# A seventh pair of weight rows as seven block products in each down projection

## The chip, the cores and the metric

The kernel runs on one core of a Trainium2 chip. The metric is the time of one execution on the device in microseconds (us); of several executions the median is given. The engines are named as in the profile: PE is TensorE (matmuls, with its weight loads as PEld), DVE is VectorE, ACT is ScalarE, POOL is GpSimd and SP is SyncE, which here only issues transfers.

## The reference

A trunk of two layers works on one sequence of 256 rows and 1024 columns, all in float32. Each layer adds half of a feed-forward network (FFN), then a mixer, then half of a second FFN. Four FFNs are therefore computed, each with 2816 hidden columns:

```python
def swiglu(x, w_gate, w_up, w_down):
    return (jax.nn.silu(x @ w_gate) * (x @ w_up)) @ w_down
...
for layer in range(DEPTH):
    h = h + 0.5 * swiglu(rms_norm(h, ffn1_norm[layer]), ...)
    hn = rms_norm(h, mix_norm[layer])
    ...
    h = h + 0.5 * swiglu(rms_norm(h, ffn2_norm[layer]), ...)
return rms_norm(h, final_norm)
```

Layer 0's mixer is attention over dilated windows beside a gated position mixing; layer 1's is causal attention. Neither is touched by the change.

## The kernel before

**Precision.** A float32 product is built from three matmuls of a shorter format: each operand is split into a high part and a low part, and high x high, high x low and low x high are summed (`mm3`, L236 to L239). A weight chunk is split on the chip: ACT writes the high part (`whi`, L93), DVE subtracts it from the raw weights and gets the low part (`wlo`, L94).

**The stream of weights.** `Stream` hands out weight chunks of 1 MB in a fixed order. A chunk is loaded into one of three `raw` buffers, split into one of four pairs of `whi` and `wlo`, used by PE and freed. `pump` loads and splits as far ahead as these buffers allow; it is called by `take` and by `free`. The code gives an order of instructions and their dependences; a scheduler then orders each engine's list by priority and by what it takes to be ready, so operations of one chunk can stand between those of another. A buffer is taken when any of its kind is free.

**An FFN.** For each pair of hidden tiles (128 hidden columns each, named by its first tile: 0, 2, ..., 20), `colwise` computes gate and up from the normalised input `xTh`, `xTl` (L391 to L393). `gated` makes `hm` (L674), and `keep` splits it into `hTh`, `hTl` (L242, L243). Then `project` computes the down projection: 11 chunks, one per pair, in the order of `DOWN`. A chunk has two tiles of 128 weight rows by 1024 columns, and the output has two row blocks of 128 rows (t = 0, 1) and two halves of 512 columns (h = 0, 1).

**Plain and mixed pairs.** A plain pair needs 2 x 2 x 2 = 8 block products of 128 x 128 by 128 x 512 (`part`, L458, L459, L462). A pair in `MIXED` takes 7 (`mixed_part`, `mm3`), after the scheme of Winograd: a pair is a 2 x 2 product of blocks, and with sums of blocks on both sides seven products do. The sums on the left are built in the gate/up loop by `mix_rows` (L718 to L721) and split into `seh`, `sel`. Those on the right are built from the weights in `split_mixed`: four sums (L103, L106 to L108) in `wx`, of which three are split into `wxh` and `wxl`. There is one `wx`, one `wxh` and one `wxl`, so the next mixed chunk can only write them when PE has done the products of the one before. For that reason the seven products alternate: in even mixed chunks the three that need `wxh`, `wxl` come first, in odd ones last.

**The end of a projection.** The last two chunks (four tiles) form the tail. For t = 0 they are computed for both halves, `n0.add` adds them to the residual `x` (L269), the mean square is taken (L278, L283) and POOL makes `rstd` (L249). While PE computes t = 1, `n0.scale` and the transposes (L342) put the normalised input of the next phase into `xTh`, `xTl`. Four products of the mixed chunks have banks of their own; `onto` adds them to `x` (L433 to L444), for t = 1 behind the mean of t = 0. In the next FFN and in layer 1's mixer the second block's transposes come after seven of the first eight steps of `rowwise` (L381 to L383).

Of the kernel before, what the change touches and what calls it, by code (L numbers as in the profile page):

```python
# [10 lines left out]
F32 = mybir.dt.float32  # L11
F32R = mybir.dt.float32r
# [4 lines left out]
D = 1024  # L17
NT = S // 128
KD = D // 128
# [8 lines left out]
RAW, SPL = 3, 4  # L28
PAIRS = 3
HEAT = 9  # L30
DOWN = [4, 6, 8, 0, 10, 12, 2, 14, 16, 18, 20]
MIXED = (6, 8, 10, 12, 14, 16)


LINE, SHIFT = 64, 16
# [3 lines left out]
class Stream:  # L39


    def __init__(self, nc, pools):
        self.nc, (self.raw_pool, self.hi_pool, self.lo_pool) = nc, pools
        self.specs, self.raws, self.parts = [], {}, {}
        self.loaded = self.split = self.done = self.next = self.mixes = 0

    def add(self, src, nk, w, shift=0, pieces=2, mixed=False):
        self.specs.append((src if isinstance(src, tuple) else (src,), nk, w, 4 if len(self.specs) < 2 else 2 if len(self.specs) < 6 else 1, shift,
                           0 if mixed else pieces))
# [45 lines left out]

    def split_mixed(self, j, raw, hi, lo):
        nc = self.nc
        lead = self.mixes % 2 == 0
        self.mixes += 1
        b11, b12, b21, b22 = (raw[:, i * 512 : (i + 1) * 512] for i in range(4))  # L100
        wx = self.mix_pool.tile([128, 3, 512], F32, name="wx")
        wxh, wxl = (self.mix_pool.tile([128, 3, 512], F32R, name=m) for m in ("wxh", "wxl"))
        nc.vector.tensor_sub(wx[:, 0, :], b22, b12)  # L103
        if not lead:
            self.split_piece(hi[:, 1024:], lo[:, 1024:], raw[:, 1024:])
        nc.vector.tensor_sub(b12, b12, b11)  # L106
        nc.vector.tensor_add(wx[:, 1, :], wx[:, 0, :], b11)
        nc.vector.tensor_sub(wx[:, 2, :], b21, wx[:, 1, :])  # L108
        if lead:
            self.split_piece(wxh, wxl, wx)  # L110
            self.split_piece(hi[:, 1024:], lo[:, 1024:], raw[:, 1024:])
        self.split_piece(hi[:, :1024], lo[:, :1024], raw[:, :1024])
        if not lead:
            self.split_piece(wxh, wxl, wx)
        self.parts[j] += (wxh, wxl)

    def pump(self):
        n = len(self.specs)
        while True:
            if self.loaded < n and self.loaded - RAW < self.split:  # L120
                self.load_one()
            elif self.split < self.loaded and self.split - SPL < self.done:
                self.split_one()
            else:
                break
# [24 lines left out]
def trunk(ctx: ExitStack, tc: tile.TileContext, a, out):  # L150
    nc = tc.nc
    x = a["x"][0]

    cp = ctx.enter_context(tc.tile_pool(name="cp", bufs=1))
    wk = ctx.enter_context(tc.tile_pool(name="wk", bufs=2))
    xp = ctx.enter_context(tc.tile_pool(name="xp", bufs=1))
# [6 lines left out]
    def bank():  # L163
        return ps.tile([128, 512], F32, name="bank")

    st = Stream(nc, (raw_pool, hi_pool, lo_pool))


    def add_cols(m, c0, w, pieces=2):
        n = CH // w  # L170
        for k in range(0, KD, n):
            st.add(m[k * 128 : (k + n) * 128, c0 : c0 + w], n, w, SHIFT if w == 256 else 0,
                   pieces if len(st.specs) > 1 else 4)

    def add_ffn(wg, wu, wd):
# [7 lines left out]
        for c in range(first, FF, 256):  # L183
            for m in (wg, wu):
                add_cols(m, c, 256)
        add_rows(wd, DOWN, MIXED)

    def add_rows(m, order, mixed=()):
        for k in order:
            st.add(m[k * 128 : (k + 2) * 128, :], 2, D, mixed=k in mixed)  # L190
# [210 lines left out]
    def project(tiles, order, nfinal, factor, nxt, after=None, mixed={}):  # L401
# [5 lines left out]
        def started(t, h):  # L407
            first = (t, h) not in begun
            begun.add((t, h))
            return first  # L410

        def mixed_part(k, w):
            i = list(mixed).index(k)
            e = [[v[:, j, :] for v in mixed[k]] for j in range(3)]
            a = [[[v[:, k + j, t, :] for v in tiles] for t in range(NT)] for j in range(2)]
            b = [[[v[:, j, h * 512 : (h + 1) * 512] for v in w[:2]] for h in range(2)] for j in range(2)]
            x = [[v[:, j, :] for v in w[2:]] for j in range(3)]
            own = [((0, 0), a[1][0], b[1][0]), ((0, 1), e[2], b[1][1]), (1, a[0][0], b[0][0]), (5, e[0], b[0][1])]
            sums = [(7, a[0][1], x[0]), (6, e[1], x[1]), ((1, 0), a[1][1], x[2])]
            for key, s, m in sums + own if i % 2 == 0 else own + sums:  # L420
                single = type(key) is int
                if key not in banks:
                    banks[key] = bank()
                first = i == 0 if single else started(*key)
                mm3(banks[key], *s, *m, first, single and i == len(mixed) - 1)
            if i < len(mixed) - 1:
                return
            p1, p5, p6, p7 = (banks[j] for j in (1, 5, 6, 7))
            x = [[xr[t][:, h * 512 : (h + 1) * 512] for h in range(2)] for t in range(NT)]
            u = st.mix_pool.tile([128, 3, 512], F32, name="wx")  # L430

            def onto(xs, v):
                nc.vector.scalar_tensor_tensor(xs, v, factor, xs, op0=ALU.mult, op1=ALU.add)  # L433

            onto(x[0][0], p1)
            nc.scalar.copy(u[:, 0, :], p1)
            nc.vector.tensor_add(u[:, 0, :], p6, u[:, 0, :])
            nc.vector.tensor_add(u[:, 1, :], p5, u[:, 0, :])
            onto(x[0][1], u[:, 1, :])

            def second_rows():
                nc.vector.tensor_add(u[:, 2, :], p7, u[:, 0, :])
                onto(x[1][0], u[:, 2, :])
                nc.vector.tensor_add(u[:, 1, :], p5, u[:, 2, :])  # L444
                onto(x[1][1], u[:, 1, :])

            late.append(second_rows)
# [16 lines left out]
        head = order[: len(order) - nfinal]  # L464
        w = None
        for i, k in enumerate(head):
            if i % 2 == 0:
                w = st.take()
            if k in mixed:
                mixed_part(k, w)  # L470
            elif k - 1 not in mixed:
                for t in range(NT):
                    part(t, k, w, i % 2, (0, 1))
            if i % 2 == 1:
                st.free()
            if after:
                after(i)
# [7 lines left out]
        for h, i in [(h, 2 * c + i) for c in range(2) for h in range(2) for i in range(2)] if after else \  # L485
                [(h, i) for h in range(2) for i in range(4)]:
            k = tail[i]
# [14 lines left out]
        with tc.issue_after(mean.ins):  # L502
            for f in () if last else late:
                f()
        if last:
            n0.final()
            rest = bank()
            for q, (c0, c1) in enumerate(((0, 512), (512, 768), (768, D))):
                b = rest[:, :256] if q == 2 else banks[1, q]
                for i, k in enumerate(tail):  # L510
                    w = [u[:, i % 2, c0:c1] for u in ws[i // 2]]
                    mm3(b[:, : c1 - c0], th[:, k, 1, :], tl[:, k, 1, :], *w, q == 2 and i == 0, k == order[-1])
                n1.last_add(q, slice(c0, D if q else c1), b, factor)
            n1.final(384)
            return
# [142 lines left out]
    def ffn(phase, begin=None):  # L658
        with ExitStack() as pools:
# [32 lines left out]
            def turn_all():  # L692
                for f in todo:
                    f()
                todo.clear()
# [19 lines left out]
            def mix_rows(k, hm):  # L715
                a11, a21, a12, a22 = (hm[:, i * 128 : (i + 1) * 128] for i in range(4))
                e = fp.tile([128, 512], F32, name="sil", bufs=2)[:, :384].rearrange("p (j c) -> p j c", j=3)
                nc.vector.tensor_add(e[:, 0, :], a21, a22)  # L718
                nc.vector.tensor_sub(a21, a11, a21)  # L719
                nc.vector.tensor_sub(e[:, 1, :], e[:, 0, :], a11)  # L720
                nc.vector.tensor_sub(e[:, 2, :], a12, e[:, 1, :])  # L721
                mixed[k] = [mq.tile([128, 3, 128], F32R, name=f"{n}{k}") for n in ("seh", "sel")]
                split(*mixed[k], e)

            if begin:
# [5 lines left out]
            else:  # L731
# [2 lines left out]
                block(1)  # L734
                finish(1)
            mq = st.mix_pool = pools.enter_context(tc.tile_pool(name="mq", bufs=1))
            mixed = {}
            for k in range(6 if begin else 2, FT, 2):
                ps2 = []
                for _ in range(2):  # L740
                    p = bank()
# [7 lines left out]
                hm = gated(*ps2)  # L749
                if k in MIXED:  # L750
                    mix_rows(k, hm)
                keep(k, hm)

            turn_all()
            project(hT, [k + j for k in DOWN for j in range(2)], 4, 0.5, phase + 1, mixed=mixed)


# [262 lines left out]
    Norm(0, 0)  # L1020
    Norm(1, 0)
    ffn(0, begin)
    ab_mixer(1)
    ffn(2)
    ffn(3)
    c_mixer(4)
# [49 lines left out]
```

## Time and profile before

| what | value |
|---|---|
| time, median of 3 runs | 925.27 us (924.82 to 926.18) |
| the profiled execution's own time | 924.85 us |
| its span | 923.1 us |
| instructions | 15780 |
| HBM read | 173.73 MB, 189 GB/s over the span |
| mixed pairs per down projection | 6 of 11 |

The span runs from the first to the last instruction; the time also holds the start and the end of the program. A row of a timeline gives the start in the span, the duration, the engine, the line, the tile written and those read, the shapes and, in brackets, how long the engine was idle before it and what released it. Matmuls and DVE operations overlap with the ones behind them, so the step from one start to the next is shorter than the duration. A group's row gives the count, the busy time in us and the mean of one in ns.

### The profile page before, as it was taken

Reading aid. Unit: us, or ns where it says so; the run is one execution under the profiler, and the core shown is the slowest. Engines: PE = TensorE matmul, PEld = TensorE weight load, DVE = VectorE, ACT = ScalarE, POOL = GpSimd, SP = SyncE. Lnnn points to the kernel's source line nnn. Section 1 sums busy time; section 2 is a strip of 40 time slices with the busy share of each in tenths; the row PEclk is TensorE's granted clock in tenths of the full one; section 3 lists DMA queues with packets and bytes.
Section 4 is the critical chain, followed back from the end, with each engine's and each line's share of the span. In section 5 each row is a group of like instructions: output and inputs, shape, how many; then the busy total and the mean of one; then the engine's idle time right before and its main releaser. Section 6 shows DMA issues by size and latency. Waiting matters only on the chain.

```text
span 923.1 us, 15780 instructions
## 1 busy us (share of the span) xinstructions
PE 915.7 (99%) x6442; PEld 843.2 (91%) x6442; DVE 691.9 (75%) x1044; ACT 538.2 (58%) x842; POOL 35.5 (4%) x53
## 2 busy tenths in 40 slices
PE   9999999999999999999999999999999999999997
PEld 8999998889889999988899999888989799999886
DVE  6886779977657566879876678898656575677797
ACT  6754555585867455546664555556756674555552
POOL 0000000000000000000000000000323100000000
PEclk9999999999999999999999999999999999999999
DMA  9885554757526766536486665473744457665351
GB/s 324 270 275 182 186 180 141 270 175 249 167 91 191 221 185 195 192 131 242 153 274 185 195 207 179 162 243 129 250 150 146 129 167 225 203 204 185 137 182 45
DMA packets 125704, 175.79 MB, mean 190 GB/s; under 512 B 3264, under 2 KB 104768, under 8 KB 125632
## 3 DMA queue, kind: packets, MB, share of 16 engines
q1 hardware_dynamic: 123952, 172.60, 57.5%
q10 hardware_dynamic: 1680, 2.19, 0.8%
q8 instruction: 50, 0.82, 0.4%
q14 instruction: 22, 0.18, 0.1%
HBM read 173.73 MB, written 1.05 MB: 189 GB/s over the span
## 4 chain that ended last, share of the span: by engine, by line
PE 99%; issue 1%; DVE 0%; ACT 0%; POOLq 0%; POOL 0%
PE bank L391 18%; PE bank L393 18%; PE bank L392 18%; PE bank L458 5%; PE bank L462 5%; PE bank L459 5%; PE bank L239 4%; PE bank L237 4%; PE bank L238 4%; PE bank L381 3%; PE bank L383 3%; PE bank L382 3%; PE bank L822 1%; PE bank L782 1%; PE bank L342 1%; PE bank L810 1%
## 5 line engine op out<-in xcount | busy, mean ns | idle before, releaser
L93 ACT ACTIVATE whi<-raw 128x1024 fp32r<-128x1024 f32 (+1 forms) x336 | 329.0, 1029 | 238.8 <-PE bank L392 102.8
L94 DVE TENSOR_TENSOR wlo<-raw,whi 128x1024 fp32r<-128x1024 f32 (+1 forms) x336 | 385.1, 1184 | 84.3 <-ACT whi L93 83.7
L391 PE MATMUL bank<-xTh,whi 128*128 128x256 f32 x1440 | 399.7, 278 | 0.0
L393 PE MATMUL bank<-xTh,wlo 128*128 128x256 f32 x1440 | 398.2, 277 | 0.0
L392 PE MATMUL bank<-xTl,whi 128*128 128x256 f32 x1440 | 398.2, 276 | 0.0
L391 PEld LDWEIGHTS bank<-xTh,whi 128*128 128x128 f32 x1440 | 270.3, 188 | 1.3 <-issue 1.2
L392 PEld LDWEIGHTS bank<-xTl,whi 128*128 128x128 f32 x1440 | 270.8, 188 | 0.1
L393 PEld LDWEIGHTS bank<-xTh,wlo 128*128 128x128 f32 x1440 | 270.5, 188 | 0.0
L674 DVE TENSOR_TENSOR hm<-sil,bank 128x512 f32<-128x512 f32 x38 | 26.1, 687 | 57.2 <-PE bank L393 57.1
L458 PE MATMUL bank<-whi,hTh 128*128 128x512 f32 x152 | 59.8, 393 | 0.0
L459 PE MATMUL bank<-wlo,hTh 128*128 128x512 f32 x152 | 59.2, 390 | 0.0
L242 ACT ACTIVATE hTh<-hm 128x512 fp32r<-128x512 f32 x39 | 24.5, 627 | 50.1 <-DVE hm L719 38.9
L462 PE MATMUL bank<-whi,hTl 128*128 128x512 f32 x152 | 51.4, 389 | 0.0
L94 DVE TENSOR_TENSOR wxl<-wx,wxh 128x1536 fp32r<-128x1536 f32 x24 | 42.1, 1755 | 11.3 <-ACT wxh L93 11.2
L381 PE MATMUL bank<-whi,xTh 128*128 128x512 f32 x112 | 44.4, 397 | 0.0
L383 PE MATMUL bank<-whi,xTl 128*128 128x512 f32 x112 | 43.8, 391 | 0.0
L382 PE MATMUL bank<-wlo,xTh 128*128 128x512 f32 x112 | 43.6, 390 | 0.0
L93 ACT ACTIVATE wxh<-wx 128x1536 fp32r<-128x1536 f32 x24 | 35.5, 1481 | 11.6 <-DVE wx L108 7.7
L249 POOL TENSOR_TENSOR rstd<-ms,half_neg 128x1 f32<-128x1 f32 x14 | 8.1, 582 | 797.2 <-DVE ms L283 792.9
L462 PEld LDWEIGHTS bank<-whi,hTl 128*128 128x128 f32 x152 | 28.5, 188 | 6.0
L459 PEld LDWEIGHTS bank<-wlo,hTh 128*128 128x128 f32 x152 | 28.6, 188 | 5.6
L458 PEld LDWEIGHTS bank<-whi,hTh 128*128 128x128 f32 x152 | 28.6, 188 | 5.5
(165 smaller groups left out, 1150.5 us busy)
## 6 DMA issues: line engine op xcount, KB each, us to landing
raw<-in_ffn_w_down SPq DMA_DIRECT2D x44, 1024.0 KB, 5.0
raw<-in_ffn_w_gate SPq DMA_DIRECT2D x38, 1024.0 KB, 5.5
raw<-in_ffn_w_up SPq DMA_DIRECT2D x38, 1024.0 KB, 5.4
raw<-in_c_w_in SPq DMA_DIRECT2D x12, 1024.0 KB, 5.4
raw<-in_ab_w_in SPq DMA_DIRECT2D x10, 1024.0 KB, 5.4
raw<-in_ffn_w_up SPq DMA_DIRECT2D x12, 512.0 KB, 6.5
raw<-in_ffn_w_gate SPq DMA_DIRECT2D x8, 512.0 KB, 4.0
raw<-in_ab_w_out SPq DMA_DIRECT2D x4, 1024.0 KB, 5.0
```

The source lines that it names most:

```text
L93: self.nc.scalar.activation(hi, raw, AF.Copy)
L94: self.nc.vector.tensor_sub(lo, raw, hi.bitcast(F32))
L237: nc.tensor.matmul(p, sh, mh, start=start, stop=False)
L381: nc.tensor.matmul(p, xh, w[0][:, k, :], start=k0 + k == 0, stop=False)
L382: nc.tensor.matmul(p, xh, w[1][:, k, :], start=False, stop=False)
L383: nc.tensor.matmul(p, xl, w[0][:, k, :], start=False, stop=k0 + k == KD - 1)
L391: nc.tensor.matmul(p, h, xh, start=k == 0, stop=False)
L392: nc.tensor.matmul(p, h, xl, start=False, stop=False)
L393: nc.tensor.matmul(p, l, xh, start=False, stop=k == KD - 1)
L458: nc.tensor.matmul(banks[t, h], sh, w[0][:, kw, cs], start=first, stop=False)
L459: nc.tensor.matmul(banks[t, h], sh, w[1][:, kw, cs], start=False, stop=False)
L462: nc.tensor.matmul(banks[t, h], sl, w[0][:, kw, cs], start=False, stop=last)
```

## The change

- `MIXED` gets pair 18, so seven of the eleven pairs take seven products. `DOWN` puts pair 4, a plain one, into the tail in its place, and 6 at the front.
- The four sums on the right become three operations: one subtraction over two blocks at a time, one addition, one subtraction. The order inside a chunk is the same in all: the sums, the second half of the chunk, the first half, the split of the sums.
- `wxh` and `wxl` have two homes, used in turn: tiles of their own (`near`), and the memory of `xTh` and `xTl` (`far`), which PE reads until the last gate/up product. `held` keeps the first chunk that needs `far` from being split until the gate/up loop has been written out (`open`).
- The order of the seven products no longer alternates: the four that need no sums of weights come first.
- After the last mixed chunk of a projection, the split of one more chunk (the second one of the next phase) is put off (`later`) until behind the mean of t = 0. The edge behind the mean binds the operations on DVE.
- Pair 6's left sums live in a buffer named `xn` of the pool `wk`, which the norms also use.

```diff
-DOWN = [4, 6, 8, 0, 10, 12, 2, 14, 16, 18, 20]
-MIXED = (6, 8, 10, 12, 14, 16)
+DOWN = [6, 0, 8, 10, 12, 2, 14, 16, 18, 4, 20]
+MIXED = (6, 8, 10, 12, 14, 16, 18)
...
     def split_mixed(self, j, raw, hi, lo):
         nc = self.nc
-        lead = self.mixes % 2 == 0
+        b11, b12, b21, _ = (raw[:, i * 512 : (i + 1) * 512] for i in range(4))
+        wx = self.mix_pool.tile([128, 3, 512], F32, name="wx")
+        wxh, wxl = self.mix_tiles[self.mixes % 2]()
         self.mixes += 1
...
-        nc.vector.tensor_sub(wx[:, 0, :], b22, b12)
-        if not lead:
-            self.split_piece(hi[:, 1024:], lo[:, 1024:], raw[:, 1024:])
-        nc.vector.tensor_sub(b12, b12, b11)
-        nc.vector.tensor_add(wx[:, 1, :], wx[:, 0, :], b11)
-        nc.vector.tensor_sub(wx[:, 2, :], b21, wx[:, 1, :])
-        if lead:
-            self.split_piece(wxh, wxl, wx)
-            self.split_piece(hi[:, 1024:], lo[:, 1024:], raw[:, 1024:])
+        nc.vector.tensor_sub(wx[:, :2, :], raw.rearrange("p (a b c) -> p a b c", a=2, b=2)[:, :, 1, :],
+                             raw[:, :1024].rearrange("p (a c) -> p a c", a=2))
+        self.split_piece(hi[:, 1024:], lo[:, 1024:], raw[:, 1024:])
+        nc.vector.tensor_add(b12, wx[:, 1, :], b11)
+        nc.vector.tensor_sub(wx[:, 2, :], b21, b12)
         self.split_piece(hi[:, :1024], lo[:, :1024], raw[:, :1024])
-        if not lead:
-            self.split_piece(wxh, wxl, wx)
+        self.split_piece(wxh, wxl, wx)
         self.parts[j] += (wxh, wxl)
+
+    def held(self):
+        return self.later or not self.specs[self.split][-1] and self.mixes % 2 and not self.open
...
-            elif self.split < self.loaded and self.split - SPL < self.done:
+            elif self.split < self.loaded and self.split - SPL < self.done and not self.held():
                 self.split_one()
...
-            own = [((0, 0), a[1][0], b[1][0]), ((0, 1), e[2], b[1][1]), (1, a[0][0], b[0][0]), (5, e[0], b[0][1])]
-            sums = [(7, a[0][1], x[0]), (6, e[1], x[1]), ((1, 0), a[1][1], x[2])]
-            for key, s, m in sums + own if i % 2 == 0 else own + sums:
+            for key, s, m in (((0, 0), a[1][0], b[1][0]), ((0, 1), e[2], b[1][1]), (1, a[0][0], b[0][0]),
+                              (6, e[1], b[0][1]), (5, e[0], x[0]), (7, a[0][1], x[1]), ((1, 0), a[1][1], x[2])):
...
             if i % 2 == 1:
+                st.later = bool(mixed) and i == len(head) - 1
                 st.free()
...
         with tc.issue_after(mean.ins):
             for f in () if last else late:
                 f()
+            if st.later:
+                st.later = False
+                st.pump()
...
-                mixed[k] = [mq.tile([128, 3, 128], F32R, name=f"{n}{k}") for n in ("seh", "sel")]
+                if k == MIXED[0]:
+                    both = wk.tile([128, D], F32, name="xn").bitcast(F32R)
+                    mixed[k] = [both[:, c : c + 384].rearrange("p (j c) -> p j c", j=3) for c in (0, 384)]
+                else:
+                    mixed[k] = [mq.tile([128, 3, 128], F32R, name=f"{n}{k}") for n in ("seh", "sel")]
...
+            st.mixes, st.open = 0, False
+
+            def near():
+                return [mq.tile([128, 3, 512], F32R, name=n) for n in ("wxh", "wxl")]
+
+            def far():
+                return [xp.tile([128, KD, NT, 128], F32R, name=n).rearrange("p k t c -> p (k t c)")[:, :1536]
+                        .rearrange("p (j c) -> p j c", j=3) for n in ("xTh", "xTl")]
+
+            st.mix_tiles = near, far
...
             turn_all()
+            st.open = True
```

More of the change, by code (lines that the diff above doesn't have):

```diff
@@ L45, in __init__ @@
         self.loaded = self.split = self.done = self.next = self.mixes = 0
+        self.open = self.later = False
     def add(self, src, nk, w, shift=0, pieces=2, mixed=False):
@@ L97, in split_mixed @@
         nc = self.nc
-        lead = self.mixes % 2 == 0
+        b11, b12, b21, _ = (raw[:, i * 512 : (i + 1) * 512] for i in range(4))
+        wx = self.mix_pool.tile([128, 3, 512], F32, name="wx")
+        wxh, wxl = self.mix_tiles[self.mixes % 2]()
         self.mixes += 1
[L100 to L103, printed above, removed]
-        if not lead:
-            self.split_piece(hi[:, 1024:], lo[:, 1024:], raw[:, 1024:])
-        nc.vector.tensor_sub(b12, b12, b11)
-        nc.vector.tensor_add(wx[:, 1, :], wx[:, 0, :], b11)
-        nc.vector.tensor_sub(wx[:, 2, :], b21, wx[:, 1, :])
-        if lead:
-            self.split_piece(wxh, wxl, wx)
-            self.split_piece(hi[:, 1024:], lo[:, 1024:], raw[:, 1024:])
+        nc.vector.tensor_sub(wx[:, :2, :], raw.rearrange("p (a b c) -> p a b c", a=2, b=2)[:, :, 1, :],
[3 more added lines that the diff above has]
+        nc.vector.tensor_sub(wx[:, 2, :], b21, b12)
         self.split_piece(hi[:, :1024], lo[:, :1024], raw[:, :1024])
-        if not lead:
-            self.split_piece(wxh, wxl, wx)
+        self.split_piece(wxh, wxl, wx)
         self.parts[j] += (wxh, wxl)
+    def held(self):
+        return self.later or not self.specs[self.split][-1] and self.mixes % 2 and not self.open
     def pump(self):
```

## The prediction

> **What bounds the kernel now.** First the view of spans and clocks, the page's part 1, and the view of what TensorE (PE) waited for:
>
> ```profile
> core 0: 923.1 us, clock 0.999
> ...
> PE 915.7 (99%) x6442; PEld 843.2 (91%) x6442; DVE 691.9 (75%) x1044; ACT 538.2 (58%) x842; POOL 35.5 (4%) x53
> ...
> PE bank L537 <- DVE warm L228: 1.1, 1, 1.1
> ```
>
> The clock is at full speed, and PE waited for another engine once, for 1.1 us at the start. All the rest, up to the last product, is PE work with no gap. So the time goes down by exactly the PE work that is removed, and up by every wait that appears. DVE's 75% is an average, so I went on to the timelines of PE and DVE inside one down projection, that of the second FFN. It begins at 395.63, which I call T0.
>
> ```profile
> 395.63 0.40 PE L458 MATMUL bank<-whi,hTh 128*128 128x512 f32 x1
> ...
> 437.59 0.39 PE L239 MATMUL bank<-whi,hTl 128*128 128x512 f32 x1
> 437.82 0.39 PE L237 MATMUL bank<-whi,seh 128*128 128x512 f32 x1
> 438.04 0.39 PE L238 MATMUL bank<-wlo,seh 128*128 128x512 f32 x1
> 438.27 0.39 PE L239 MATMUL bank<-whi,sel 128*128 128x512 f32 x1
> 438.50 0.39 PE L237 MATMUL bank<-wxh,hTh 128*128 128x512 f32 x1
> 438.72 0.39 PE L238 MATMUL bank<-wxl,hTh 128*128 128x512 f32 x1
> ```
>
> Matmuls take 0.39 us but start 0.227 apart (437.59 to 438.50, four steps), so a block product of three is 0.68 us, a mixed chunk (7 products) 4.76 and a plain one (8) 5.44. The row at 438.50 is the first product of pair 16 that needs `wxl`. DVE's timeline of the same stretch:
>
> ```profile
> 395.90 0.69 DVE L674 TENSOR_TENSOR hm<-sil,bank 128x512 f32<-128x512 f32 x1 [0.53 <-PE bank L393]
> 396.82 2.36 DVE L94 TENSOR_TENSOR wlo<-raw,whi 128x1024 fp32r<-128x1024 f32 x2 [0.23 <-ACT whi L93]
> 399.10 0.69 DVE L243 TENSOR_TENSOR hTl<-hm,hTh 128x512 fp32r<-128x512 f32 x1
> 402.44 1.23 DVE L94 TENSOR_TENSOR wlo<-raw,whi 128x1024 fp32r<-128x1024 f32 x1 [2.66 <-ACT whi L93]
> 404.92 1.76 DVE L94 TENSOR_TENSOR wxl<-wx,wxh 128x1536 fp32r<-128x1536 f32 x1 [1.25 <-ACT wxh L93]
> ...
> 413.79 1.75 DVE L94 TENSOR_TENSOR wxl<-wx,wxh 128x1536 fp32r<-128x1536 f32 x1
> 415.58 0.69 DVE L103 TENSOR_TENSOR wx<-raw 128x512 f32<-128x512 f32 x1
> 416.30 0.69 DVE L106 TENSOR_TENSOR raw<-raw 128x512 f32<-128x512 f32 x1
> 416.91 0.69 DVE L107 TENSOR_TENSOR wx<-wx,raw 128x512 f32<-128x512 f32 x1
> 417.63 0.69 DVE L108 TENSOR_TENSOR wx<-raw,wx 128x512 f32<-128x512 f32 x1
> 418.24 2.35 DVE L94 TENSOR_TENSOR wlo<-raw,whi 128x1024 fp32r<-128x1024 f32 x2
> 420.51 1.75 DVE L94 TENSOR_TENSOR wxl<-wx,wxh 128x1536 fp32r<-128x1536 f32 x1
> 422.30 0.69 DVE L103 TENSOR_TENSOR wx<-raw 128x512 f32<-128x512 f32 x1
> ...
> 428.25 1.75 DVE L94 TENSOR_TENSOR wxl<-wx,wxh 128x1536 fp32r<-128x1536 f32 x1
> 429.92 1.22 DVE L94 TENSOR_TENSOR wlo<-raw,whi 128x1024 fp32r<-128x1024 f32 x1
> 431.05 0.69 DVE L103 TENSOR_TENSOR wx<-raw 128x512 f32<-128x512 f32 x1
> ...
> 436.13 1.76 DVE L94 TENSOR_TENSOR wxl<-wx,wxh 128x1536 fp32r<-128x1536 f32 x1
> ```
>
> From 404.92 DVE never rests. Pair 16's `wxl` ends at 437.89, and PE uses it at 438.50: 0.61 us to spare. **PE sets the time, but in the down projections DVE is only just ahead of it.** Four such stretches, one per FFN, are where the change works.
>
> **The change part by part.** *Product removed.* Pair 18 takes 7 products in place of 8, in four FFNs: 4 x 0.68 = 2.72 us less. Chunk 4 only moves from the front to the tail. That is certain as PE work.
>
> *DVE's work.* Costs are steps from one start to the next: a 512-wide operation 0.60 (416.30 to 416.91), 0.72 where the next one needs its result (415.58 to 416.30), a 1024-wide one 1.13 (2.35 less 1.22), a `wxl` 1.68 (428.25 to 429.92) and 1.79 where the next waits for its end (420.51 to 422.30). A mixed chunk was 4 x 0.60 + 2.27 + 1.68 = 6.35. With the two sums in one operation (not in this trace; from one 1024-wide row up to two 512-wide ones, 1.13 to 1.20; I take 1.13, the same number of elements) it is 6.28. A plain chunk is 2.27. So the seventh mixed chunk adds 6.28 - 2.27 = 4.0 us of DVE work and the merging takes 0.07 x 6 = 0.4 back from the others, while PE goes through the stretch 0.68 us sooner.
>
> The Trainium skill, page "VectorE: DVE Perf Modes", section "The DRAIN you can't avoid", says that the next operation starts only when the pipe of the one before is empty; merging would then save 2 x 0.69 - 1.22 = 0.16 us a chunk. The rows speak against it, with starts 0.60 apart at 0.69 each. By the page DVE would be 0.5 us earlier at pair 18 than I reckon below, and the sum 2 us lower.
>
> *Two homes.*
>
> ```profile
> 403.40 1.49 ACT L93 ACTIVATE wxh<-wx 128x1536 fp32r<-128x1536 f32 x1 [0.99 <-PE bank L239]
> ```
>
> Now 8's `wxh` waits for the products of 6, and DVE with it: 0.23 + 2.66 + 1.25 = 4.1 us of idle time in the rows from 396.82 to 404.92. With a second home in `xT`, 8's `wxh` waits only for the last gate/up product, at T0. Of the 4.1 us about 1 stays (`wxh` takes 1.49 after T0, and DVE has just `hm` to do), so some 3 us are won.
>
> *When is pair 18 due?* Six mixed chunks and two plain ones before it, and four products that need no sums: 6 x 4.76 + 2 x 5.44 + 2.72 = 42.2 us after T0. DVE's list until its `wxl` is done: 1.7 until 8's `wxl` can start, 1.68 for it, 0.60 for `hTl`, five mixed chunks (10, 12, 14, 16, 18) 31.4, chunk 2 2.27: 37.65. To this come two things that are not fixed:
>
> ```profile
> L94 DVE TENSOR_TENSOR wlo<-raw,whi x15: 1217/1219/1226, 396.8 to 434.8; 128x1024 fp32r<-128x1024 f32 x15
> ```
>
> These are the `wlo` pieces before 16's `wxl`. Chunks 0, 10, 12, 2, 14 and 16 need 12 of the 15. The other three belong to the two chunks after them: the order of issue fills a moment in which the next sum is not ready by a whole 1.13 us piece (429.92, ahead of the `L103` at 431.05). The same filling is possible with chunks 4 and 20: none to four pieces, 0 to 4.5 us; I take 3.5 pieces, 4.0. And the steps inside a chunk wait: 0.11 and 0.12 for a result of DVE's own, and for ACT, whose `whi` of the first half now follows the second sum and whose `wxh` (1.49) is last, with one 1.13 piece to cover it (not in this trace): 0.2 to 0.7 a chunk, five chunks, 1.0 to 3.5; I take 2.4, the middle. Sum 37.65 + 4.0 + 2.4 = 44.05, which is **1.9 us late**; the ends are in time (38.65, 3.5 us early) and 3.5 us late (45.65). A second way to the same: 0.61 to spare, + 3.0 + 0.4 - 4.0 - 0.68 = -0.7, less the new waits for ACT, which the four short sums of a chunk cover today. PE then waits at 18, once per FFN: 4 x 1.9 = 7.6 us.
>
> *The split behind the mean.* The second chunk of the next phase (two `wlo`, 2.27 us) goes behind the mean of the first row block.
>
> ```profile
> 448.15 0.21 DVE L283 TENSOR_SCALAR ms<-ss 128x1 f32<-128x1 f32 x1 [0.79 <-ACT xn L278]
> ...
> 452.66 1.13 DVE L354 SCALAR_TENSOR_TENSOR xTl<-bank,gT,xTh 128x128 fp32r<-128x128 f32 x4 [0.53 <-ACT xTh L352]
> ...
> 455.18 0.21 DVE L283 TENSOR_SCALAR ms<-ss 128x1 f32<-128x1 f32 x1 [0.28 <-ACT xn L278]
> 456.12 0.49 DVE L322 TENSOR_SCALAR xn<-x,rstd 128x512 f32<-128x512 f32 x1 [0.73 <-POOL rstd L249]
> ...
> 457.12 1.03 PE L342 MATMUL bank<-ident,xn 128*128 128x128 f32 x8
> ```
>
> It clears DVE ahead of the mean, but no PE wait is there to be won. Behind the mean DVE has 0.53 us idle before the second mean, and `xn` of the second block is done 0.51 before its transposes: room for 1.0 of the 2.27, and 0.28 + 0.73 more while DVE waits for ACT and POOL, if the order puts a piece there. So it is 0 to 1.2 us late at the starts of the third FFN and of layer 1's mixer (elsewhere the turn comes later or no phase follows). I take 0.3 each, 0.6, which is what is left when all the idle time is used.
>
> *Nothing* for what these rows hide:
>
> ```profile
> 374.14 0.69 DVE L674 TENSOR_TENSOR hm<-sil,bank 128x512 f32<-128x512 f32 x1 [2.17 <-PE bank L393]
> ...
> 377.75 0.69 DVE L103 TENSOR_TENSOR wx<-raw 128x512 f32<-128x512 f32 x1
> ...
> L243 DVE TENSOR_TENSOR sel<-sil,seh 128x384 fp32r<-128x384 f32 x24 | 13.2, 552 | 0.0
> L718 DVE TENSOR_TENSOR sil<-hm 128x128 f32<-128x128 f32 x24 | 7.0, 292 | 0.8
> ...
> raw<-in_ffn_w_down SPq DMA_DIRECT2D x44, 1024.0 KB, 5.0
> ```
>
> That is: `mix_rows` of 18 (four operations of 0.29 and one of 0.55, 1.7 us of DVE in the gate/up loop, where a single wait is longer; uncovered, 8 would be as much later), the loads (same bytes; those held leave at about T0 + 10 and take 5.0 us to land, while DVE reaches them after T0 + 20), `xn` as home of pair 6's left sums (free again after the first chunk), and the bank order (7 of 8 asked for at once, the last at T0 + 4.1; `hm` frees the last of the gate/up loop by 396.59).
>
> **Sum:** 924.85 - 2.72 + 7.6 + 0.6 = 930.3 from the profiled run. The median of the three is 0.42 above that run, so I say 930.5.
>
> **The rivals.** *Faster:* pair 18's splits come ahead of those of 4 and 20, at most one piece is put in front, and DVE is done by 37.65 + 1.1 + 2.4 = 41.2, before 42.2. Then only the product goes: 925.27 - 2.72 = 922.5. For it speaks that PE waited for none of the 24 mixed chunks of before; against it the three pieces put in front there. It decides at about 2 pieces. Chance 0.28. *No change:* 18 is late by 0.2 to 1.1 us, about what one product gives: 923.4 to 927.1, chance 0.14. *Much slower:* the hold (8 not split before T0) really keeps 8's sums and `wlo` off DVE's idle time in front of T0. Then 6.28 - 1.68 = 4.6 us more stand in the list, 18 is 6.5 late, and the time is about 925 + 4 x (6.5 - 0.68) = 948. Against it: DVE takes up mixed sums well ahead of their turn now (the `L103` at 377.75, 17.9 us before T0), and a hold in program order need not be one in time. Chance 0.06.
>
> **How the numbers follow.** Forecast 0.52: its own range is 927 (late by 1.2: 924.85 - 2.72 + 4.8) to 937 (late by 3.5 and 1.2 twice would be 938.5, all at their ends at once). The smallest difference that this measurement can tell is about 0.2%, 1.85 us. Faster 0.28, same 0.14, slower 0.52 + 0.06 = 0.58. Cases of both signs count, so the range reaches down to the faster rival and up to most of the forecast: 922.2 to 936.5.
>
> **What will show it.** PE's waits should list the products of `mixed_part` waiting for DVE's `wlo` or `wxl`, in four places, at the last mixed chunk, longest first; `wxl` of 18 should end after T0 + 42.2, with pieces of 4 and 20 in front; PE's instructions should be 12 fewer. If PE waits for nothing, the filling was reckoned wrong and the time is 922.5. If the first waits come at pair 8 or 10, the hold is to blame. A wait at the transposes after the second mean is the moved split.

## The result, and the profile after

The changed kernel takes 933.13 us (median of 5 runs, 932.79 to 933.51), against 925.05 for the one before it in the same comparison: a ratio of 1.0085, 95% interval 1.0072 to 1.0099. It is slower by 8.1 us, although PE has 12 instructions less to do. Times and ratios here and below leave out three single executions far above the rest: 950.84 and 1029.4 us in two of the experiments, at a granted clock of 0.948 and 0.85, and 4290.95 us in one of the kernel of before. First the spans, part 1 of the page, and what PE waited for (us in all, times, the longest):

```profile
core 0: 931.6 us, clock 0.999
...
PE 916.9 (98%) x6430; PEld 838.6 (90%) x6430; DVE 715.3 (77%) x1056; ACT 544.8 (58%) x850; POOL 35.9 (4%) x53
...
PE bank L235 <- ACT whi L94: 2.2, 2, 1.3
PE bank L381 <- DVE xTl L352: 1.8, 3, 0.7
PE bank L570 <- ACT whi L94: 1.4, 2, 0.9
PE bank L538 <- DVE warm L226: 1.1, 1, 1.1
PE bank L340 <- ACT xn L318: 0.9, 2, 0.5
```

The clock is the same. Before, PE waited once; now it waits in `mixed_part` (L235), at the transposes of a block (L340) and at the first rows of the next phase (L381). The list holds only the longer waits. The whole is seen when PE's timeline is cut at the same instructions in both kernels: the first product of each down projection, the first transpose behind it, and the last product.

| stretch of PE's timeline | before | after | more |
|---|---|---|---|
| start to the first down projection | 126.92 | 127.79 | 0.87 |
| four down projections, to the transposes (the last to the start of its last product) | 54.52, 54.43, 54.43, 55.82 | 54.97, 54.92, 55.64, 56.43 | 2.76 |
| behind them, to the next down projection | 214.19, 123.56, 232.66 | 215.54, 124.87, 234.15 | 4.15 |
| last product to the end of the span | 6.6 | 7.3 | 0.7 |

The sum is 8.4 us, the difference of the two spans. The projections have 2.72 us of products less, so PE waits 2.76 + 2.72 = 5.5 us in them, and 4.15 behind them. The 0.87 at the start does not follow the change: in the ten kernels of the experiments, whose PE work up to there is the same, this stretch ends between 126.8 (a kernel with seven pairs) and 128.1 (one with six).

The second FFN's projection starts at 398.31 (T0). DVE's timeline around pair 18:

```profile
429.37 0.69 DVE L107 TENSOR_TENSOR wx<-raw 128x512 f32<-128x512 f32 x1
430.47 1.22 DVE L95 TENSOR_TENSOR wlo<-raw,whi 128x1024 fp32r<-128x1024 f32 x1 [0.41 <-ACT whi L94]
431.85 1.76 DVE L95 TENSOR_TENSOR xTl<-wx,xTh 128x1536 fp32r<-128x1536 f32 x1 [0.15 <-ACT xTh L94]
433.52 1.22 DVE L95 TENSOR_TENSOR wlo<-raw,whi 128x1024 fp32r<-128x1024 f32 x1
434.66 1.22 DVE L103 TENSOR_TENSOR wx<-raw 128x1024 f32<-128x1024 f32 x1
435.79 1.22 DVE L95 TENSOR_TENSOR wlo<-raw,whi 128x1024 fp32r<-128x1024 f32 x1
436.93 0.68 DVE L106 TENSOR_TENSOR raw<-wx,raw 128x512 f32<-128x512 f32 x1
437.65 0.69 DVE L107 TENSOR_TENSOR wx<-raw 128x512 f32<-128x512 f32 x1
438.25 3.49 DVE L95 TENSOR_TENSOR wlo<-raw,whi 128x1024 fp32r<-128x1024 f32 x3
441.66 1.75 DVE L95 TENSOR_TENSOR wxl<-wx,wxh 128x1536 fp32r<-128x1536 f32 x1
```

The low part written to `xTl` is pair 16's, in the far home. Pair 18's chain is the `L103` at 434.66, the two short sums and the `wxl` at 441.66, which ends at 443.41, T0 + 45.1; it was due at T0 + 42.2. Between them stand pieces of chunks 4 and 20, and the waits for ACT (0.41, 0.15) are there as reckoned. All the `wlo` pieces of that stretch:

```profile
L95 DVE TENSOR_TENSOR wlo<-raw,whi x16: 1216/1218/1227, 399.5 to 440.5; 128x1024 fp32r<-128x1024 f32 x16
```

Twelve belong to 10, 12, 2, 14, 16 and 18, so all four of chunks 4 and 20 came first. `wxl` is 2.9 us late, but PE loses only 1.2 us in this projection. PE's own timeline shows why:

```profile
438.97 0.39 PE L237 MATMUL bank<-whi,sel 128*128 128x512 f32 x1
439.20 0.39 PE L455 MATMUL bank<-whi,hTh 128*128 128x512 f32 x1
439.67 0.50 PE L235 MATMUL bank<-whi,hTh 128*128 128x512 f32 x1
...
441.19 0.40 PE L235 MATMUL bank<-wxh,seh 128*128 128x512 f32 x1
...
442.82 0.39 PE L459 MATMUL bank<-whi,hTl 128*128 128x512 f32 x1
...
443.74 0.39 PE L236 MATMUL bank<-wxl,seh 128*128 128x512 f32 x1
```

L455 and L459 are products of the tail. The order of issue has put them between those of pair 18, so PE works on chunks 4 and 20 while DVE finishes 18. What is gained there is missing later: the tail's sums end later, and so does the mean.

The longest wait in `mixed_part` is in the third FFN, 1.33 us, and it is for ACT's `whi` and not for a low part:

```profile
620.71 0.50 PE L235 MATMUL bank<-whi,hTh 128*128 128x512 f32 x1 [1.33 <-ACT whi L94]
```

The chain of work that ended last, in the same stretch, shows what made it late, and the mean behind it:

```profile
610.26 1.24 DVE wlo L95
611.51 6.08 DMA raw<-in_ffn_w_down
617.70 1.07 ACT whi L94
618.79 2.37 DVE wlo L95 x2
621.18 5.35 DMA raw<-in_c_w_in
626.63 0.39 ACT whi L94
627.17 0.62 ACT whi L94
627.79 0.48 ACT wx L433
```

Twice here DVE ends a piece that frees a `raw` buffer, a load leaves at once, and ACT goes on only when its chunk has landed, 6.08 and 5.35 us later. In ACT's list the pieces of chunk 20 stand ahead of the first half of 18, for which PE waits, and pieces of the next phase ahead of the copy of the sums (L433), which the mean needs. On the page the whole chain has a share of 4% for DMA and 6% for DVE; before, DMA was not in it and DVE had 0%. So DVE's lateness also comes back by way of the loads that it sets off.

Behind the mean of the second FFN:

```profile
451.51 0.21 DVE L281 TENSOR_SCALAR ms<-ss 128x1 f32<-128x1 f32 x1 [0.79 <-ACT xn L276]
...
452.24 1.22 DVE L95 TENSOR_TENSOR wlo<-raw,whi 128x1024 fp32r<-128x1024 f32 x1
...
454.57 1.21 DVE L95 TENSOR_TENSOR wlo<-raw,whi 128x1024 fp32r<-128x1024 f32 x1
...
456.31 0.60 DVE L352 SCALAR_TENSOR_TENSOR xTl<-bank,gT,xTh 128x128 fp32r<-128x128 f32 x2
```

Both put-off pieces stand ahead of the first `xTl`, for which PE waits at L381 (0.5 us in this FFN). The mean is at T0 + 53.2, 0.7 later than before (448.15 - 395.63 = 52.5).

### The profile page after: what moved, and what is told of

The parts are those of the page before. It is cut to its first block, busy times and chain, and to the rows that moved or that the text cites. A ratio compares the mean times of both kernels' runs of the same rounds, so it can differ in the third digit from the quotient of the medians.

```text
span 931.6 us, 15771 instructions
## 1 busy us (share of the span) xinstructions
PE 916.9 (98%) x6430; PEld 838.6 (90%) x6430; DVE 715.3 (77%) x1056; ACT 544.8 (58%) x850; POOL 35.9 (4%) x53
## 4 chain that ended last, share of the span: by engine, by line
PE 85%; DVE 6%; DMA 4%; ACT 2%; issue 2%; SPq 0%; POOL 0%; POOLq 0%; ACTq 0%; DVEq 0%
PE bank L389 18%; PE bank L390 18%; PE bank L391 18%; PE bank L235 3%; PE bank L237 3%; PE bank L236 3%; PE bank L381 3%; DVE wlo L95 3%; PE bank L379 3%; PE bank L380 3%; PE bank L455 3%; PE bank L459 3%; PE bank L456 3%; DMA raw<-in_ffn_w_down 1%; ACT whi L94 1%
## 5 line engine op out<-in xcount | busy, mean ns | idle before, releaser
L455 PE MATMUL bank<-whi,hTh 128*128 128x512 f32 x120 | 47.2, 394 | 0.0
L456 PE MATMUL bank<-wlo,hTh 128*128 128x512 f32 x120 | 46.8, 390 | 0.0
L381 PE MATMUL bank<-whi,xTl 128*128 128x512 f32 x112 | 44.4, 396 | 1.8 <-DVE xTl L352 1.8
L459 PE MATMUL bank<-whi,hTl 128*128 128x512 f32 x120 | 41.5, 389 | 0.0
L103 DVE TENSOR_TENSOR wx<-raw 128x1024 f32<-128x1024 f32 x28 | 34.1, 1218 | 0.1
L350 ACT ACTIVATE xTh<-bank,gT 128x128 fp32r<-128x128 f32 x80 | 23.3, 373 | 12.2 <-PE bank L340 7.5
L241 DVE TENSOR_TENSOR hTl<-hm,hTh 128x512 fp32r<-128x512 f32 x39 | 26.9, 688 | 4.4 <-ACT hTh L240 4.4
L95 DVE TENSOR_TENSOR wxl<-wx,wxh 128x1536 fp32r<-128x1536 f32 x16 | 28.1, 1754 | 1.2 <-ACT wxh L94 0.8
L352 DVE SCALAR_TENSOR_TENSOR xTl<-bank,gT,xTh 128x128 fp32r<-128x128 f32 x80 | 22.6, 342 | 7.9 <-ACT xTh L350 7.8
```

The source lines that it names most:

```text
L95: self.nc.vector.tensor_sub(lo, raw, hi.bitcast(F32))
L103: nc.vector.tensor_sub(wx[:, :2, :], raw.rearrange("p (a b c) -> p a b c", a=2, b=2)[:, :, 1, :], raw[:, :1024].rearrange("p (a c) -> p a ...
L381: nc.tensor.matmul(p, xl, w[0][:, k, :], start=False, stop=k0 + k == KD - 1)
L455: nc.tensor.matmul(banks[t, h], sh, w[0][:, kw, cs], start=first, stop=False)
L456: nc.tensor.matmul(banks[t, h], sh, w[1][:, kw, cs], start=False, stop=False)
L459: nc.tensor.matmul(banks[t, h], sl, w[0][:, kw, cs], start=False, stop=last)
```

## The experiments

All ratios are to the kernel of before, timed on the same chip. "Projections", "behind" and "end" are the rows of the table above, as differences from before.

**Is it the put-off split?** The split of the next phase's second chunk goes back to its place.

```diff
-                st.later = bool(mixed) and i == len(head) - 1
```

> The changed kernel without the put-off split: the second chunk of the next phase is split where the free puts it, as before. Theory A (the two pieces of wlo behind the mean are what xTl and the second turn wait for): the waits of PE for xTl and xn at the start of the next phase (1.30 + 1.25 + 1.42 us against before) go away, nothing comes in their place ahead of the mean, time 929.2 us. Rival C (the put-off was needed because DVE is late at the mean): the two pieces delay the add and the mean of the first row block, and PE waits 1 to 2 us more at the first transposes in three places: 931 to 935 us.

Measured: 932.79 us, ratio 1.0082 (1.0069 to 1.0096), the same as with the put-off. Projections 7.66 more (with 2.72 less to do, so 10.4 us of waits), behind 1.01 less.

```profile
PE bank L235 <- ACT whi L94: 2.6, 4, 1.3
PE bank L340 <- ACT xn L318: 1.5, 2, 0.9
```

The waits for `xTl` are gone and those at the first transposes are longer: the mean of the same projection is now at T0 + 55.0. Theory A was wrong that nothing would take their place, and rival C right. **The put-off moves about 5 us of waiting from ahead of the mean to behind it, and saves nothing.**

**Is it the seventh pair?** The changed code, with the pairs and the order of before:

```diff
-DOWN = [6, 0, 8, 10, 12, 2, 14, 16, 18, 4, 20]
-MIXED = (6, 8, 10, 12, 14, 16, 18)
+DOWN = [4, 6, 8, 0, 10, 12, 2, 14, 16, 18, 20]
+MIXED = (6, 8, 10, 12, 14, 16)
```

> The changed kernel with the six mixed pairs and the order of the chunks of before; two homes, merged sums, hold and put-off split stay. Theory A (the seventh pair makes DVE late): no wait of PE at the last mixed chunk; what is left is the put-off split alone, 925.1 + 4.0 = 929 us. Rival B (the new order of the sums, the hold of the second mixed chunk or the second home are late by themselves): PE still waits in mixed_part, 5 us in all with the put-off's 4: 933 us or more.

> Six mixed pairs and the chunk order of before, two homes, merged sums, no put-off. Theory D: DVE has less to do than before (0.07 us a chunk and 3 us of idle time at the front won), so PE waits nowhere, 925.1 to 925.5 us; the 2.7 us by which the same kernel with the put-off was slower were the put-off's. Rival (the new order of sums itself costs): 926.5 us or more, with waits in the down projections.

Measured: 927.81 us with the put-off (ratio 1.0028, 1.0017 to 1.0040) and 925.75 without (1.0005, 0.9996 to 1.0013). With the put-off, the stretches behind the projections are 0.61, 0.62 and 0.77 longer; without it they are within 0.01 of before. PE does not wait in `mixed_part` in either, and the projections are 0.13 longer each. So the homes, the new order of sums and the hold cost next to nothing by themselves, the put-off costs 2.0 us where it is not needed, and the lateness in the projections comes with the seventh pair and the order of chunks that goes with it. Theory A had the put-off at twice its price here.

**What are the two homes and merged sums worth?** The kernel of before with only the seventh pair and the new order of chunks, in one home and with four sums (pair 6's left sums in `xn`):

```diff
-DOWN = [4, 6, 8, 0, 10, 12, 2, 14, 16, 18, 20]
-MIXED = (6, 8, 10, 12, 14, 16)
+DOWN = [6, 0, 8, 10, 12, 2, 14, 16, 18, 4, 20]
+MIXED = (6, 8, 10, 12, 14, 16, 18)
```

> The kernel of before with only the seventh pair and the new order of chunks: one home of wxh and wxl, four sums, no put-off; pair 6's left sums in xn. Theory A (one home makes DVE idle for some 3 us at the front of every down projection, which it cannot make up): PE waits about 3 us more in each of four FFNs than with two homes, time 925 - 2.7 + 4 x 5 = 942 us (935 to 948). Rival (the homes and the merged sums give nothing): 930 us, as after without the put-off.

Measured: 951.2 us, ratio 1.0280 (1.0266 to 1.0294). PE waits mostly at the first transposes:

```profile
PE bank L342 <- ACT xn L320: 13.5, 3, 4.7
```

So two homes, merged sums and the new order of products, which this run leaves out together, are worth 18 us to seven pairs, more than theory A's 12 or so. The granted clock was 0.989 in all five executions, against 0.998 and 0.999 in those of before; what part of the 18 us that is, no run shows.

**Is it the order on DVE?** In the changed kernel, no `wlo` piece of a later chunk may be issued on DVE ahead of the `wxl` of 18.

```diff
+        with self.tc.issue_after(self.edge.ins):
+            return self.nc.vector.tensor_sub(lo, raw, hi.bitcast(F32))
...
+        last = self.split_piece(wxh, wxl, wx)
+        if self.mixes == len(MIXED):
+            self.edge = last
```

> The changed kernel, but no wlo piece of a later chunk may be issued on DVE ahead of the wxl of the last mixed chunk, 18. Theory A (pieces of 4 and 20 put in front make 18 late, by three to four times 1.13 us): 18's wxl ends about 3.4 us earlier against its products, PE's waits at 18 go away in all four FFNs; 4 and 20 are then due at once behind it, some 0.5 us late. Time 930 us (929 to 931). Rival (DVE's whole load is too much, whatever the order): the wait moves to the pieces of 4 and 20 in the tail and the time stays at 933 us within 1.

Measured: 937.33 us, ratio 1.0138 (1.0124 to 1.0151). `wxl` of 18 ends at T0 + 41.6 in the last three projections (T0 is the start of each), in time and 3.5 to 4.3 us earlier than in the changed kernel, and no wait in `mixed_part` is left:

```profile
PE bank L347 <- ACT xn L325: 4.3, 3, 1.6
PE bank L388 <- DVE xTl L359: 4.2, 3, 1.6
```

The waits have gone to the transposes and to the next phase. Where no phase follows, in the last FFN, the projection is 55.21 us, 0.61 shorter than before, but the stretch from the last product to the end of the span is 2.1 longer. **The size of theory A's effect was right, and its conclusion wrong: this order moved the waits and made the time 4 us longer.** This gave theory D: DVE has too much to do between the start of a projection and the turn of its first block, in whatever order. This run kept the put-off; the same order without it was run in the last FFN alone (the last experiment).

**Less work for DVE, on POOL.** Without the put-off; six `wlo` pieces of the plain chunks, or the merged sum of every mixed chunk, go to POOL.

```diff
-            self.split_piece(hi[:, a : a + h], lo[:, a : a + h], raw[:, a : a + h])
+            self.split_piece(hi[:, a : a + h], lo[:, a : a + h], raw[:, a : a + h],
+                             nc.gpsimd if j in self.pool else nc.vector)
```

> The changed kernel without the put-off, and with the wlo pieces of the plain chunks 2, 4 and 20 of each down projection subtracted on POOL in place of DVE: six pieces of 1.13 us, 6.8 us of DVE work less per FFN, nothing else. Theory D, formed on the first four runs (it is DVE's whole load between the start of a projection and the turn of the first row block that is too large, by 1.5 to 2.5 us an FFN, whatever the order): all waits of PE at 18, at the first transposes and at xTl go, and the time is 922.5 to 923.5 us, faster than before. Rival E (POOL and DVE slow each other down, or POOL takes over 5 us a piece): the pieces are late, PE waits for wlo from POOL, 930 us or more.

```diff
-        nc.vector.tensor_sub(wx[:, :2, :], ...)
+        nc.gpsimd.tensor_sub(wx[:, :2, :], ...)
```

> The changed kernel without the put-off, and the merged sum of each mixed chunk (128x1024) on POOL in place of DVE: 7 x 1.13 = 7.9 us of DVE work less per FFN, but POOL's time comes into the chain from one wx to the next. Theory D: time 922.5 to 924 us if POOL takes up to 2.3 us for it. Rival F (the chain from wxl of one chunk to wxl of the next is what binds, not DVE's load): the time stays at 933 us or goes up.

Measured: 963.37 us (ratio 1.0409, 1.0395 to 1.0423) and 968.04 (1.0461, 1.0448 to 1.0475). POOL's row of the first, then two rows of DVE from it (shortest, median and longest, in ns):

```profile
L97 POOL TENSOR_TENSOR wlo<-raw,whi 128x1024 fp32r<-128x1024 f32 x24 | 73.2, 3071 | 601.1 <-ACT whi L96 601.1
```

```profile
L105 DVE TENSOR_TENSOR wx<-raw x28: 1216/1219/3312, 103.0 to 930.6; 128x1024 f32<-128x1024 f32 x28
L108 DVE TENSOR_TENSOR raw<-wx,raw x28: 684/692/2773, 104.3 to 934.0; 128x512 f32<-128x512 f32 x28
```

The same two groups in the changed kernel, as means:

```profile
L103 DVE TENSOR_TENSOR wx<-raw 128x1024 f32<-128x1024 f32 x28 | 34.1, 1218 | 0.1
L106 DVE TENSOR_TENSOR raw<-wx,raw 128x512 f32<-128x512 f32 x28 | 19.3, 688 | 0.5
```

A piece takes 3.07 us on POOL and 1.22 on DVE. Most of DVE's sums keep their time, but eight of the 28 merged ones take 3.3 us and eight of the short ones 2.7 to 2.8, two of each per FFN: 33 us more in all, where the 24 pieces took 27 off. In this run DVE is held up beside POOL, as rival E had it, though POOL takes under 5 us. The Trainium skill, page "SBUF — State Buffer", section "Who interferes with whom", says that a DVE instruction with two inputs in SBUF contends with a GpSimd instruction that reads SBUF. These rows agree.

In the second run DVE's operations keep their times; there DVE waits for POOL's sums:

```profile
L106 DVE TENSOR_TENSOR raw<-wx,raw 128x512 f32<-128x512 f32 x28 | 19.4, 692 | 66.2 <-POOL wx L103 66.2
```

That is 66.2 us of waiting for 28 sums, which took 1.13 us each on DVE. So neither run tests theory D: POOL gave DVE more to wait for than it took off. For the second run rival F is not excluded by its time alone.

**Less work for DVE, on ACT.** To take work off DVE and change nothing else, ACT writes a copy of the raw weights as the low part of plain chunks, so that part of the result is not computed: six pieces per FFN, then two. Without the put-off.

```diff
+        if light:
+            self.nc.scalar.activation(lo, raw, AF.Copy)
+        else:
+            self.nc.vector.tensor_sub(lo, raw, hi.bitcast(F32))
```

> Seven pairs without the put-off. The low parts of the plain chunks 2, 4 and 20 are not the difference: ACT writes a copy of the raw weights there, so DVE has six pieces of 1.13 us (6.8 us) less to do per FFN, ACT six more, and PE's work is the same. Theory D (DVE's whole load in the projection): DVE was late by 3.0, 3.0, 3.0 and 1.6 us in the four down projections of the run without the put-off; 6.8 us less is more than that, so no wait is left and the time is 922.5 to 923.2 us. Rival G (the chain wx, wxh, wxl from one mixed chunk to the next is what is late): 18 stays late, 928 us or more.

> As the run before, but only chunk 4's two pieces (2.3 us of DVE per FFN) go to ACT. Theory D: 3.0 - 2.3 = 0.7 us of wait is left in three down projections, none in the last, time about 924.8 us. Rival G: as without the change, 930 to 933 us.

Measured: 922.49 us with six pieces less (ratio 0.9969, 0.9958 to 0.9981), which is 2.7 us under the 925.2 of before, just the products removed. What PE waited for is left at the start alone, and DVE rests behind 18:

```profile
PE bank L576 <- ACT whi L96: 1.5, 2, 1.0
PE bank L544 <- DVE warm L233: 1.1, 1, 1.1
```

```profile
434.37 1.76 DVE L100 TENSOR_TENSOR wxl<-wx,wxh 128x1536 fp32r<-128x1536 f32 x1 [0.15 <-ACT wxh L96]
437.75 0.69 DVE L437 SCALAR_TENSOR_TENSOR x<-bank,x 128x512 f32<-128x512 f32 x1 [1.63 <-PE bank L244]
```

With two pieces less: 926.26 us (1.0011, 1.0002 to 1.0020). The last projection is 0.61 shorter than before, the three others 0.55, 1.03 and 0.34 longer, 1.0 to 1.7 us of waits each and not 0.7; all that is left is at the first transposes. In the second of them ACT waits 1.10 and 1.39 us for weights of the next phase to land ahead of its copy of the sums, so the loads have a share there, which was not tested by itself. Rival G is out: the chain of `wx` is as long in both runs and 18 is in time. Both runs take away DVE's work and, with it, the late loads that DVE's pieces set off; a fourth `raw` buffer or another order on ACT, which would change the loads and the copy alone, was not run.

**A version for the last FFN only.** Six pairs in the first three FFNs, seven in the last with the pieces behind 18, no put-off:

```diff
+MIXED = [(6, 8, 10, 12, 14, 16), (6, 8, 10, 12, 14, 16, 18)]
...
+        add_rows(wd, DOWN[last], MIXED[last])
```

> A version that may beat both: six pairs and the old chunk order in the first three FFNs, seven in the last, whose projection is followed by no split of a next phase; there the pieces of chunks behind 18 may not be issued on DVE ahead of 18's wxl; two homes, no put-off; computes the reference. Theory D: the last projection was 0.6 us shorter than before in the run with the pieces behind 18, the rest is as in the run of six pairs in place: 925.75 - 0.7 = 925.0 us, within 0.1% of before. Rival: the last projection is late too, 926 us or more.

Measured: 926.86 us, ratio 1.0018 (1.0009 to 1.0026). The last projection is 0.61 shorter as expected, but from PE's last product to the end of the span it is 1.8 us longer: the final norms wait for DVE. The gain is given back within the same FFN. No version here that computes the reference beat the kernel of before.

## Why the prediction was right, and where it was off

- *PE bound, product removed:* right. With DVE relieved the time falls by 2.7 us, the 2.72 reckoned.
- *DVE only just ahead:* right, and it is the cause of the result, shown by the two runs with less for DVE. How the lateness reaches PE was not all foreseen: the prediction put the loads at nothing, but loads that DVE sets off late are links of the chain (6.08 and 5.35 us in the third FFN). How much of the time they make up stays open.
- *18 late by 1.9 us, 7.6 in all:* right in kind. `wxl` of 18 is later than reckoned (2.9 us in the FFN shown, with all four pieces in front), yet the waits in the projections are 5.5 us, because PE takes products of the tail first. The prediction took PE's order as that of the code. Its sign, waits for `wlo` or `wxl` at 18 in four places, did not come: `mixed_part` waits in the last two FFNs, for ACT's `whi` (1.33 and 0.91 us), and in the first two the listed waits of the projections are at the transposes (0.46 and 0.48). The 0.61 us to spare before was read at the first product's start; the matmul that reads `wxl` starts at 438.72, 0.83 behind its end, which changes no term of the sum.
- *The faster rival, "pair 18's splits come ahead":* its condition did not come by itself, all four pieces were in front. Where an experiment made it hold, the `wxl` was in time, but the time went up to 937.3 and not down to 922.5. The sum stopped at 18, where it should have run on to the mean and the turn.
- *The put-off, 0.6 us:* this is the term that was mis-sized. It measured 4.15 us, over 1.3 at each of three places, layer 0's mixer among them, where the prediction saw nothing due. The pieces were not spread over the idle time: both stand ahead of the first `xTl`. Part of it is DVE's backlog, since the same put-off costs 2.0 us with six pairs. Taken out, it gives nothing back, because the wait then comes ahead of the transposes.
- *The end of the kernel:* not reckoned; 0.7 us.
- *The sum:* 933.13 us against 930.5 lies in the range in part by luck. The waits in the projections came out 2.1 us under their term and those behind them 3.55 over theirs, so the two errors partly cancel.
- *Much slower by the hold:* out. The six-pair runs keep the hold and do not wait.
- *The seventh pair's two mitigations:* the prediction gave the second home "some 3 us" per FFN and the merged sum 0.07 a chunk. Without both, and with the old order of products, the kernel takes 18 us more, 4.6 per FFN, so they are worth more than that, with the reserve about the clock above.
- *Merging and the pipe:* the Trainium skill, page "VectorE: DVE Perf Modes", section "The DRAIN you can't avoid", adds that an operation which is not held starts earlier, which the prediction left out. The merged sum was followed 1.13 us later (434.66 to 435.79) at 1.22 us of duration, as reckoned from the rows.

## What to carry to other kernels

An engine that is busy 75% of the span can be full in the very stretch where work is added, so reckon its list in that stretch up to the last thing that waits for it, not to the first. Here putting a part off moved the wait (933.1 against 932.8 us) and reordering made it longer (937.3). The test was to take work off the engine, even with a part of the computation left out for it, before a better order was looked for. The list also counts for the loads: a buffer freed late is filled late.

## What was not expected of the hardware

POOL beside DVE was much dearer than POOL's own time. A 128x1024 subtraction took 3.07 us there, and in the run with the pieces on POOL some of DVE's sums took up to 2.77 us in place of 0.69 and up to 3.31 in place of 1.22, while most kept their time. The profiled runs with POOL also show a lower granted clock, 0.982 and 0.987 against 0.999; the runs do not tell why.
